# Preparation of the next group in sixteen pieces over a round trip, more streamed products beside scores and joins, a gate by banks

## The chip, the cores and the metric

The kernel runs on one core of one Trainium2 chip. The metric is the device time of one execution in microseconds (us). An execution has five engines and their queues: TensorE (PE, its weight loads PEld), VectorE (DVE), ScalarE (ACT), GpSimd (POOL), and SyncE (SP), which issues most of the DMA transfers.

## What is computed

One layer of a hybrid model on 256 tokens of width 2048, all in float32. A wide product `x @ w_in` gives the inputs of two mixers and two gates: a gated linear attention (GLA, 4 heads) and an RWKV-7 recurrence (16 heads of 64, forward and backward). Their outputs go through up-projections, are gated, summed and projected out, then comes a layer norm, and then a feed-forward layer with 16 experts that choose their tokens. Cut to what matters here:

```python
cols = x @ w_in                       # 2048 x 10592 weights
y_gla = gla_branch(q, k, v, g, af, ab, ...)    # ends in  * silu(g)
y_rw = rwkv_branch(rw_p, ...)
merged = sigmoid(gate_gla) * (y_gla @ w_up_gla) + sigmoid(gate_rw) * (y_rw @ w_up_rwkv)
x = layer_norm(ALPHA * x + merged @ w_out)
x = layer_norm(ALPHA * x + expert_choice_ffn(x, w_router, w1, w3, w2))

def rwkv_branch(...):                 # for each head, forward and backward
    w = exp(-0.606531 * sigmoid(w0 + tanh(xw) @ w_up));  a = sigmoid(a0 + xa @ a_up)
    kk = normalize(k * k_k);  k = k * (1 + (a - 1) * k_a);  a_vec, b_vec = -kk, kk * a
    # for each token:  S = S * w + (S @ a_vec) b_vec^T + v k^T ;  y = S @ r
```

## The kernel before

**Two phases.** The first phase computes everything up to the first layer norm. The second runs the experts, whose weights it reads from memory into rings of buffers that are taken from the first phase's pools when these close.

**Streamed products.** The dense products of the first phase are a list of jobs (`rw`, `lora`, `gqk`, `gv`, `gg`, `gate`, the up-projections, the output projection), in this order. For each block of 128 rows of weights, `split` (L241 on ScalarE, `tt` through L65 on VectorE) turns the raw float32 tile `wraw` into two reduced-precision parts `whi` and `wlo`, and three matmuls use them: L278 to L280 with 256 columns where the job gives its output transposed, L287 to L289 with 512 where it does not. In all jobs together 3888 such matmuls run. `wraw` has three buffers of two blocks; `fetch` (L224, on SyncE's queue) asks for the next pair of blocks as soon as the last one is split. `whi` and `wlo` have nine buffers each, and the splits run six blocks ahead. When a job's matmuls have ended, its `evac` generator is advanced by `drain`, one step for each block of the following job.

**The chain.** The two mixers are a chain of small matmuls and operations on VectorE and ScalarE: `rwkv_group` for four groups of four heads, then two GLA pairs. The chain is a generator, and `run_chain` sets the order of the program: at each `yield w` it lets the stream put `w` us worth of streamed products (by its own cost numbers) behind what the chain has just issued. All engines get their instructions in that order.

**One group.** `rwkv_group` starts with a transpose of the values (L774), then come the masked scores (matmuls L789, masks through L65 into `am`), eight halves with a `yield` after each. Then a first trip through device memory, the solution of small triangular systems on VectorE (the loop that ends at L870), and a second trip: SyncE stores the result to `sc2` (L873) and loads it back in another layout into `nt` (L878), both waiting for data. This second trip is the *round trip* here; `yield SUBST` (20.4 us of products) stands in it. Then VectorE transposes the blocks (L883), and the *joins* follow: matmuls L891, L898, L912 and L933, with copies and a second transpose (L902) between them. Then the *scan* over four chunks (L945 to L1003), and its output.

**What runs beside it.** `beside` wraps another generator so that `side(us)` advances it by `us` of its own yields. `side` is the preparation of the next group (`rwkv_prep`): matmuls L686, L693 and L703, then on ScalarE exponentials and logarithms (L688 to L742), on VectorE two running sums over time (L722 and L724), halves of the key product (L737), products (L745), and eight products of keys with decays, into `kr` (tag `t8`) and `nk` (tag `t8b`), with `yield 1.80` after each four. It is advanced in the triangle loop (`w * SPREAD`), in the round trip by `side(SIDE1)` with SIDE1 = 7.5, then in the scan (SIDE2), and a last `side(1e9)` at the group's end issues what is left, with its streamed products. `before` is the output part of the group before. Group 3 has no preparation to carry.

## Time and profile before

| What | Value |
|---|---|
| median of 3 runs | 1877.7 us (1876.88 to 1881.24) |
| the profiled execution | 1876.1 us, its span 1874.4 us |
| TensorE busy | 1607.3 us, 86% of the span, 11369 matmuls |
| VectorE busy | 775.6 us, 41%, 1407 instructions |
| ScalarE busy | 540.1 us, 29%, 1077 instructions |
| memory read, written | 543.20 MB, 16.78 MB; 299 GB/s over the span |
| transfers of the weights | `ring_a` 180, `ring` 139, `t8b` 39 of 1 MB each; `wraw` 112 of 512 KB and 96 of 256 KB on `w_in` |
| chain of work that ended last | DMA 41%, PE 32%, DVE 9%, ACT 2% |

The profile is one execution of the program, taken by the hardware profiler. A page lists busy times, the span in 40 slices, and groups of instructions; other views list the waits of an engine by the instruction that released it, the timeline of an engine, and tables by stretch. L-numbers are lines of the kernel. In a row, `out<-in` are the names of the tiles, and the "granted clock" is TensorE's as a share of 2.4 GHz, so that 0.50 is 1.2 GHz. The groups of rows further down say which view they are from.

### The profile page before, as it was taken

The numbers are of one execution on the slowest core, as the hardware profiler recorded it, in microseconds if no ns is written. First come the engines' busy times: TensorE is split into PE (matmuls) and PEld (weight loads), VectorE is DVE, ScalarE is ACT, GpSimd is POOL, SyncE is SP. The second block draws the span as 40 slices with busy tenths as digits, with TensorE's granted clock in tenths as the row PEclk, the third lists the DMA queues.
The fourth block names the chain that finished last, engine by engine and source line by source line (L and its number), as shares of the span: only waits on it lengthen the run. The fifth ranks groups of instructions, "written<-read, shape, count | busy, mean of one in ns | idle before, by whom it ended". The sixth has DMA issues, their size and how long they took to land.

```text
span 1874.4 us, 27915 instructions
## 1 busy us (share of the span) xinstructions
PE 1607.3 (86%) x11369; PEld 961.4 (51%) x11369; DVE 775.6 (41%) x1407; ACT 540.1 (29%) x1077; POOL 21.0 (1%) x45
## 2 busy tenths in 40 slices
PE   8999999989999999999796898668996679966684
PEld 8988877778777778888631233112331113411122
DVE  6777675757657885765531302111012110112114
ACT  5565454445546765544310001000010000100001
POOL 0000000000000000000000000000000000000001
PEclk9999999999999999999898899999999899998988
DMA  7757264552736658788899999999999999999997
GB/s 203 218 160 207 75 166 137 147 158 77 192 110 205 177 151 275 267 300 280 328 417 405 421 421 421 421 421 421 421 420 421 421 420 421 421 420 421 415 395 210
DMA packets 215426, 561.81 MB, mean 300 GB/s; under 512 B 49848, under 2 KB 110706, under 8 KB 171906
## 3 DMA queue, kind: packets, MB, share of 16 engines
q1 hardware_dynamic: 214000, 559.80, 80.9%
q8 instruction: 89, 1.46, 0.3%
q10 hardware_dynamic: 1298, 0.24, 0.1%
q14 instruction: 39, 0.32, 0.1%
HBM read 543.20 MB, written 16.78 MB: 299 GB/s over the span
## 4 chain that ended last, share of the span: by engine, by line
DMA 41%; PE 32%; DVE 9%; ACT 2%; issue 2%; SPq 1%; DVEq 0%; ACTq 0%
DMA ring_a<-in_w_dram 18%; DMA ring<-in_w_dram 17%; PE mm L287 6%; PE mm L288 5%; PE mm L289 5%; DMA t8b<-in_w_dram 5%; PE mm L1502 3%; PE mm L1462 2%; DVE wlo L65 2%; DVE t L65 2%; PE mm L278 2%; PE mm L279 1%; PE mm L280 1%; DVE t2p L65 1%; ACT whi L241 1%
## 5 line engine op out<-in xcount | busy, mean ns | idle before, releaser
L65 DVE TENSOR_TENSOR wlo<-wraw,whi 128x512 fp32r<-128x512 f32 (+2 forms) x480 | 308.5, 664 | 202.3 <-ACT whi L241 200.5
L241 ACT ACTIVATE whi<-wraw 128x512 fp32r<-128x512 f32 (+2 forms) x480 | 275.4, 606 | 181.3 <-DMA wraw<-in_w_in_dram 58.3
L278 PE MATMUL mm<-x,whi 128*128 128x256 f32 x688 | 207.6, 302 | 3.2 <-ACT whi L241 3.2
L1462 PE MATMUL mm<-ring_a,x 128*32 128x512 f32 x776 | 155.6, 671 | 57.4 <-DMA ring_a<-in_w_dram 57.4
L279 PE MATMUL mm<-x,whi 128*128 128x256 f32 x688 | 196.9, 286 | 0.0
L280 PE MATMUL mm<-x,wlo 128*128 128x256 f32 x688 | 196.8, 286 | 0.1
L1474 DVE TENSOR_SCALAR sig<-sig 64x512 f32<-64x512 f32 x16 | 6.8, 424 | 435.0 <-ACT sig L1472 435.0
L287 PE MATMUL mm<-whi,x 128*128 128x512 f32 x384 | 163.0, 424 | 4.6 <-DVE shd L65 4.6
L1502 PE MATMUL mm<-ring_a,hid 128*32 128x512 f32 (+1 forms) x560 | 152.0, 585 | 8.8 <-DMA ring_a<-in_w_dram 7.4
L1462 PE MATMUL mm<-ring,x 128*32 128x512 f32 x592 | 117.3, 687 | 48.7 <-DMA ring<-in_w_dram 48.6
L288 PE MATMUL mm<-wlo,x 128*128 128x512 f32 x384 | 154.1, 401 | 0.0
L289 PE MATMUL mm<-whi,x 128*128 128x512 f32 x384 | 153.4, 400 | 0.0
L65 DVE TENSOR_TENSOR x<-x,ax 128x512 f32<-128x512 f32 (+2 forms) x36 | 22.3, 626 | 289.8 <-PE ax L1509 289.8
L278 PEld LDWEIGHTS mm<-x,whi 128*128 128x128 f32 x688 | 133.7, 194 | 10.0 <-ACT whi L241 3.6
L279 PEld LDWEIGHTS mm<-x,whi 128*128 128x128 f32 x688 | 134.1, 195 | 2.3 <-issue 2.2
L280 PEld LDWEIGHTS mm<-x,wlo 128*128 128x128 f32 x688 | 133.9, 195 | 0.6 <-DVE wlo L65 0.6
L1472 ACT ACTIVATE sig<-mm 64x512 f32<-64x512 f32 x16 | 9.4, 588 | 407.8 <-PE mm L1462 407.8
L1502 PE MATMUL mm<-ring,hid 128*32 128x512 f32 (+2 forms) x456 | 120.7, 556 | 6.2 <-DMA ring<-in_w_dram 5.5
L1462 PEld LDWEIGHTS mm<-ring_a,x 128*32 128x32 f32 x776 | 30.1, 115 | 159.3 <-DMA ring_a<-in_w_dram 108.6
L1502 PEld LDWEIGHTS mm<-ring_a,hid 128*32 128x32 f32 x560 | 42.9, 113 | 107.7 <-issue 84.3
L1506 ACT ACTIVATE eo<-mm 128x512 f32<-128x512 f32 (+2 forms) x18 | 9.9, 550 | 295.4 <-PE mm L1502 282.5
L1462 PEld LDWEIGHTS mm<-ring,x 128*32 128x32 f32 x592 | 23.0, 118 | 132.7 <-DMA ring<-in_w_dram 91.9
(336 smaller groups left out, 2165.7 us busy)
## 6 DMA issues: line engine op xcount, KB each, us to landing
ring_a<-in_w_dram SPq DMA_DIRECT2D x180, 1024.0 KB
ring<-in_w_dram SPq DMA_DIRECT2D x139, 1024.0 KB
wraw<-in_w_in_dram SPq DMA_DIRECT2D x112, 512.0 KB
t8b<-in_w_dram SPq DMA_DIRECT2D x39, 1024.0 KB
wraw<-in_w_in_dram SPq DMA_DIRECT2D x96, 256.0 KB
wraw<-in_w_out_dram SPq DMA_DIRECT2D x24, 512.0 KB
ring_a<-in_w_dram SPq DMA_DIRECT2D x18, 512.0 KB
wraw<-in_w_up_rwkv_dram SPq DMA_DIRECT2D x16, 512.0 KB
```

The source lines that it names most:

```text
L65: dve.tensor_tensor(out_, a, b, op=op)
L241: act(hi, raw, AF.Copy)
L278: mm(o, whi[:, sl], hi(k), start=(st0 and cb % 2 == 0), stop=False, skip_group_check=True)
L279: mm(o, whi[:, sl], lo(k), start=False, stop=False, skip_group_check=True)
L280: mm(o, wlo[:, sl], hi(k), start=False, stop=st1, skip_group_check=True)
L287: mm(o, hi(k)[:, sl], whi, start=st0, stop=False)
L288: mm(o, hi(k)[:, sl], wlo, start=False, stop=False)
L289: mm(o, lo(k)[:, sl], whi, start=False, stop=st1)
L1462: mm(ps[32 * q:32 * q + 32, :], xe[:, kb, e4 * 32:e4 * 32 + 32], wt[q // 2][:, k, (q % 2) * 512:(q % 2) * 512 + 512], start=(kb == 0), sto ...
L1472: act(sg_[up_], ps[lo_], AF.Exp, scale=-1.0)
L1502: mm(ps[32 * e4:32 * e4 + 32, 0:m], hids[e4][:, fb % 4, fb // 4, :], wt[e4][:, j, c - c0:c - c0 + m], start=(fb == 0), stop=(fb == F // 12 ...
L1506: act(eo[:, 0:m], ps[:, 0:m], AF.Copy)
```

## The change

Five edits, and none adds or removes a streamed product, a transfer of weights or an operation of the preparation:

- The `yield SUBST + side(SIDE1)` in the round trip becomes sixteen yields of `SUBST / 16 + side(SIDE1 / 16)`, and SIDE1 goes from 7.5 to 20.4. The preparation, all but its last steps, is issued in that place, interleaved with the streamed products, in steps of 1.275 us.
- The last yields of the preparation go from 1.80 to 2.90 (two of them).
- The yield after each half of the scores goes from 0.41 to 0.75, and three yields between the joins from 1.00 to 1.60, 2.20 and 1.60.
- The step of the job `gg` that turns the gate into `silu` works on a whole bank (512 columns, in place in `shd`) instead of on halves (256 columns, in `shs`, with the product in `shd`): 2 x 4 steps of `drain` instead of 4 x 4 for each of the two jobs.
- In the preparation, the two ScalarE exponentials of `a_` are issued behind both matmuls instead of one behind each.

The diff:

```diff
-    SPREAD, SIDE1, SIDE2, POST, SUBST = 0.30, 7.50, 0.81, 1.35, 20.40
+    SPREAD, SIDE1, SIDE2, POST, SUBST, PIECES = 0.30, 20.40, 0.81, 1.35, 20.40, 16
...
             def ev(b, s=s):
-                for i in range(4):
-                    if i % 2 == 0:
-                        t = S([128, 2, T], "shd", 2)
-                    ge = S([128, T], "shs", 2)
-                    o = b[i // 2][:, i % 2 * T:i % 2 * T + T]
-                    act(ge, o, AF.Exp, scale=-1.0)
+                for i in range(2):
+                    ge = S([128, 512], "shd", 2)
+                    act(ge, b[i], AF.Exp, scale=-1.0)
                     yield
                     cap(ge)
                     yield
                     sigm(ge)
                     yield
-                    tt(t[:, i % 2, :], o, ge, OP.mult)
+                    tt(ge, b[i], ge, OP.mult)
                     yield
-                    if i % 2:
-                        c0 = s * 512 + i // 2 * 256
-                        load(gg_dram[c0:c0 + 256, :].rearrange("(a p) t -> p a t", p=128), t)
+                    c0 = s * 512 + i * 256
+                    load(gg_dram[c0:c0 + 256, :].rearrange("(a p) t -> p a t", p=128), ge.rearrange("p (a t) -> p a t", a=2))
...
         for p in range(2):
             mm(ps[:, p * T:p * T + T], lw[0:64, 1, p * 128:p * 128 + 128], xab[0:64, :], start=True, stop=True)
+        for p in range(2):
             act(a_[:, p, :], ps[:, p * T:p * T + T], AF.Exp, bias=na0[:, p0 + p:p0 + p + 1], scale=-1.0)
...
             tt(nk[:, d, :, :, 64:128], v4(k2), eN[:, :, :, inc], OP.mult)
-            yield 1.80
+            yield 2.90
...
-                    yield 0.41 + before(POST)
+                    yield 0.75 + before(POST)
...
-        yield SUBST + side(SIDE1)
+        for _ in range(PIECES):
+            yield SUBST / PIECES + side(SIDE1 / PIECES)
...
         act(cu[:, 0], pv, AF.Copy)
-        yield 1.00
+        yield 1.60
...
             dve.transpose(flat(us[32 * d:32 * d + 32]), flat(cu[96 * d:96 * d + 32, 1]))
-        yield 1.00
+        yield 2.20
...
         dve.tensor_copy(c1[tq[1]], pv[tq[1]])
-        yield 1.00
+        yield 1.60
```

Where the streamed products stand in TensorE's order, counted in the two programs (L-numbers of before; the groups are numbered from 0):

| Place | Before | After |
|---|---|---|
| ahead of the first scores, all | 804 | 825 |
| scores of group 0, one gap after another (L789) | 6, 9, 9, 6 | 12, 15, 15, 15 |
| group 0's round trip | L686, L686, L693, L703 at once, then 192 | L686, 12, L686, 12, L693, 24, L703, 144 |
| behind the joins L891, L898, L912, L933, group 0 | 9, 9, 12, 3 | 15, 18, 15, 6 |
| the same, group 1 | 6, 3, 6, 3 | 9, 9, 6, 3 |
| the same, group 2 | 9, 9, 9, 6 | 15, 18, 15, 6 |
| the same, group 3 | 6, 3, 6, 3 | 9, 9, 6, 3 |
| between the scan and the next L774, groups 0, 1, 2 | 42, 21, 45 | 9, 6, 3 |
| ahead of the last matmul of the second GLA pair (L1197), all | 2901 | 2958 |

VectorE in group 0's round trip, from the triangle to the transposes of the trip (L883 before, L881 after; `shs` and `shd` are the shift of an `rw` job), before:

```order
L65 TENSOR_TENSOR wlo<-wraw,whi 128x512 x12
L65 TENSOR_TENSOR shs<-ppad 128x256
L333 SCALAR_TENSOR_TENSOR shd<-shs,der,shd 128x256
L65 TENSOR_TENSOR wlo<-wraw,whi 128x512
L65 TENSOR_TENSOR shs<-ppad 128x256
L333 SCALAR_TENSOR_TENSOR shd<-shs,der,shd 128x256
L65 TENSOR_TENSOR wlo<-wraw,whi 128x512 x2
L65 TENSOR_TENSOR shs<-ppad 128x256
L333 SCALAR_TENSOR_TENSOR shd<-shs,der,shd 128x256
L65 TENSOR_TENSOR wlo<-wraw,whi 128x512
L883 STREAM_TRANSPOSE t_2196<-t_2196 64x512 x2
L65 TENSOR_TENSOR shs<-ppad 128x256
```

And after (`t_2460` is the preparation's `kkn`, `t2p` its decays, `t8b` its `nk`, `ld` its loaded inputs):

```order
L65 TENSOR_TENSOR shs<-ppad 128x256
L333 SCALAR_TENSOR_TENSOR shd<-shs,der,shd 128x256
L65 TENSOR_TENSOR wlo<-wraw,whi 128x512
L65 TENSOR_TENSOR shs<-ppad 128x256
L333 SCALAR_TENSOR_TENSOR shd<-shs,der,shd 128x256
L65 TENSOR_TENSOR wlo<-wraw,whi 128x512
L65 TENSOR_TENSOR t_2575<-t_2460,t2p 128x8x64
L65 TENSOR_TENSOR t_2575<-ld,t2p 128x8x64
L65 TENSOR_TENSOR t8b<-t_2511,t2p 128x8x64
L65 TENSOR_TENSOR t8b<-t_2461,t2p 128x8x64
L65 TENSOR_TENSOR wlo<-wraw,whi 128x512 x3
L881 STREAM_TRANSPOSE t_2271<-t_2271 64x512 x2
```

Four of the eight products with the decays, and the two halves and two products that they need, now stand ahead of the transposes of the trip, among the splits; before, all stood behind the joins.

ScalarE in the same place, before (L705 and L712 are the preparation's logarithm and exponential of the decays, L892 is the copy behind the first join):

```order
L698 ACTIVATE t_2214<-ld,prm 128x256 x2
L705 ACTIVATE t_2199<-t_2199,c_one 128x512 x2
L712 ACTIVATE t2p<-t_2199 128x8x64 x2
L332 ACTIVATE shd<-ppad,der 128x256
L241 ACTIVATE whi<-wraw 128x512 x11
L327 ACTIVATE ppad<-mm 128x2x256
L241 ACTIVATE whi<-wraw 128x512
L332 ACTIVATE shd<-ppad,der 128x256
L241 ACTIVATE whi<-wraw 128x512
L332 ACTIVATE shd<-ppad,der 128x256
L241 ACTIVATE whi<-wraw 128x512
L327 ACTIVATE ppad<-mm 128x2x256
```

And after, up to the second pass over the decays (L702, which ends a row ahead, and L709 are those two; the copy behind the first join is L890 and stands further down):

```order
L709 ACTIVATE t2p<-t_2274 128x8x64 x2
L241 ACTIVATE whi<-wraw 128x512
L713 ACTIVATE t_2324<-t_2324 128x512
L714 ACTIVATE t_2318<-t_2318,c_one 128x512
L241 ACTIVATE whi<-wraw 128x512
L723 ACTIVATE t_2324<-t_2324 128x512
L724 ACTIVATE t_2318<-t_2318 128x512
L327 ACTIVATE ppad<-mm 128x2x256
L241 ACTIVATE whi<-wraw 128x512
L729 ACTIVATE t2p<-t2p 128x520 x2
L735 ACTIVATE t_2461<-t_2318,der,prm 128x256 x2
L739 ACTIVATE t2p<-t2p 128x520 x2
```

The ten operations from L713 to L739 now stand ahead of the first join's copy, among the splits; before, they stood behind the joins (L716 to L742).

ScalarE in the job `gg0`, before (L416 is the exponential, L341 and L342 the logarithm and the exponential of `sigm`):

```order
L416 ACTIVATE shs<-mm 128x256
L241 ACTIVATE whi<-wraw 128x512 x2
L975 ACTIVATE av<-ax 64x4x64
L341 ACTIVATE shs<-shs,c_one 128x256
L342 ACTIVATE shs<-shs 128x256
L241 ACTIVATE whi<-wraw 128x512 x2
L975 ACTIVATE av<-ax 64x2x2x64
L416 ACTIVATE shs<-mm 128x256
L241 ACTIVATE whi<-wraw 128x512 x2
L341 ACTIVATE shs<-shs,c_one 128x256
L342 ACTIVATE shs<-shs 128x256
L241 ACTIVATE whi<-wraw 128x512 x2
```

And after (L413 is the exponential):

```order
L413 ACTIVATE shd<-mm 128x512
L241 ACTIVATE whi<-wraw 128x512 x2
L341 ACTIVATE shd<-shd,c_one 128x512
L342 ACTIVATE shd<-shd 128x512
L241 ACTIVATE whi<-wraw 128x512 x2
L413 ACTIVATE shd<-mm 128x512
L241 ACTIVATE whi<-wraw 128x512
```

One row on 512 columns stands for two on 256, and the second bank's exponential comes earlier among the splits.

## Rows read from the trace of the kernel before

**Rows 1.** The page's second part, the span in 40 equal slices: busy tenths.

```profile
PE   8999999989999999999796898668996679966684
...
DMA  7757264552736658788899999999999999999997
```

**Rows 2.** Waits of PE, 0 to 900 us: total us, times, longest us.

```profile
PE ax L789 <- DVE am L65: 6.8, 7, 2.0
...
PE mm L287 <- DVE shd L65: 4.6, 1, 4.6
...
PE ax L703 <- ACT t L698: 4.1, 3, 1.4
...
PE ax L789 <- DVE t8b L65: 3.2, 1, 3.2
```

**Rows 3.** Stretches: us; PE, PEld, DVE, ACT, POOL busy; clock; DMA; GB/s.

```profile
119.00:130.60 11.60, 10.77 (x95) 9.39 (x95) 11.26 (x21) 1.95 (x4) 0.11 (x1) 0.85 0.45 134
...
153.10:160.40 7.30, 5.28 (x13) 2.20 (x12) 6.24 (x14) 4.76 (x11) 0.00 (x0) 0.82 0.45 127
...
160.40:164.50 4.10, 4.10 (x21) 4.10 (x20) 3.73 (x7) 3.52 (x7) 0.00 (x0) 0.50 0.73 169
...
164.50:185.00 20.50, 20.50 (x173) 20.40 (x172) 12.21 (x22) 9.31 (x17) 0.00 (x0) 1.00 0.78 220
...
185.00:200.40 15.40, 13.53 (x435) 11.93 (x434) 7.27 (x15) 5.65 (x12) 0.00 (x0) 0.78 0.29 88
...
229.10:244.00 14.90, 11.11 (x99) 9.60 (x100) 13.81 (x26) 4.88 (x10) 0.00 (x0) 0.89 0.35 95
...
298.80:312.40 13.60, 12.10 (x420) 8.90 (x419) 6.28 (x13) 5.29 (x11) 0.00 (x0) 0.87 0.28 91
...
340.40:351.50 11.10, 9.59 (x83) 7.25 (x82) 10.44 (x19) 5.18 (x10) 0.00 (x0) 1.00 0.39 116
...
404.80:421.10 16.30, 13.37 (x435) 11.92 (x434) 6.73 (x13) 5.52 (x12) 0.00 (x0) 0.77 0.23 69
...
451.40:464.00 12.60, 9.38 (x90) 7.86 (x89) 12.29 (x24) 4.45 (x10) 0.52 (x1) 1.00 0.33 89
...
500.00:505.90 5.90, 5.82 (x14) 4.57 (x15) 0.62 (x2) 0.00 (x0) 0.00 (x0) 0.50 0.88 226
...
518.30:534.50 16.20, 13.45 (x419) 10.26 (x418) 6.68 (x13) 5.24 (x11) 0.00 (x0) 0.79 0.30 97
...
725.00:750.00 25.00, 25.00 (x111) 20.60 (x110) 11.55 (x20) 12.44 (x22) 0.00 (x0) 1.00 0.89 308
```

**Rows 4.** Timeline of DVE, 158 to 184 us: start, us, instruction, [idle before].

```profile
172.39 1.29 DVE L65 TENSOR_TENSOR wlo<-wraw,whi 128x512 fp32r<-128x512 f32 x2 [4.17 <-ACT whi L241]
...
183.30 0.71 DVE L883 STREAM_TRANSPOSE t<-t 64x512 f32<-64x512 f32 x1
```

**Rows 5.** Timeline of SyncE's queue, 155 to 190 us, in the same columns.

```profile
164.15 1.31 SPq L878 DMA_DIRECT2D t<-sc  x2
...
166.58 15.47 SPq L224 DMA_DIRECT2D wraw<-in_w_in_dram  x14
```

**Rows 6.** DVE's splits, 173.7-183.3, 284.3-297.6, 391.5-401.95 us: busy, mean ns, idle before.

```profile
L65 DVE TENSOR_TENSOR wlo<-wraw,whi 128x512 fp32r<-128x512 f32 x8 | 5.3, 687 | 1.7 <-ACT whi L241 1.6
...
L65 DVE TENSOR_TENSOR wlo<-wraw,whi 128x512 fp32r<-128x512 f32 x10 | 6.9, 691 | 6.5 <-ACT whi L241 6.4
...
L65 DVE TENSOR_TENSOR wlo<-wraw,whi 128x512 fp32r<-128x512 f32 x9 | 6.0, 689 | 4.5 <-ACT whi L241 4.5
```

**Rows 7.** DVE, 158 to 236 us, shapes apart: busy, mean ns, idle before.

```profile
L722 DVE TENSOR_TENSOR_SCAN t2p<-rstr,t2p 128x520 f32<-128x520 f32 x1 | 1.2, 1243 | 0.0
...
L737 DVE SCALAR_TENSOR_TENSOR t<-ld,prm,t 128x256 f32<-128x256 f32 x2 | 0.9, 470 | 0.0
...
L65 DVE TENSOR_TENSOR t8b<-t,t2p 128x512 f32<-128x512 f32 x4 | 2.6, 684 | 0.0
```

**Rows 8.** Timeline of ACT, 505 to 522 us, columns as in group 4.

```profile
505.96 0.63 ACT L241 ACTIVATE whi<-wraw 128x512 fp32r<-128x512 f32 x1 [6.47 <-DMA wraw<-in_w_in_dram]
```

## The prediction

> **What bounds the kernel now.** I read the slices of the page first [rows 1]. Up to about 900 us TensorE is busy almost without a break; after that the DMA engines are, with the experts' weights. The change touches the first part alone. Whatever that part loses or gains, the second part starts as much later or earlier: its weights go into buffers that come free when the first part ends. So I ask one thing: what TensorE does in the first part that is not matmul time at full clock. Its work there is fixed, since the same 3888 streamed products and the same chain matmuls run before and after. The time can move only by its waits and by stretches at half clock.
>
> The waits by releaser [rows 2] show where it waits: on the masked scores, on the preparation's squares, once on the gate's product, once on the first group's operands. The table by stretch [rows 3] gives their size: 119.0 to 130.6, 229.1 to 244.0, 340.4 to 351.5 and 451.4 to 464.0 are the scores of the four groups; 153.1 to 160.4 is the preparation of the next group, issued in one piece; 160.4 to 164.5 follows it at a granted clock of 0.50, which is 1.2 instead of 2.4 GHz; the four stretches from 185.0, 298.8, 404.8 and 518.3 are the joins, from the first join matmul to the first matmul of the scan. A streamed product costs 0.118 us where 256 columns move (20.50 us for 173) and 0.225 us where 512 do (25.00 for 111).
>
> A group is also a chain: scores, a first trip through memory, the triangle on VectorE, a second trip, transposes, joins, scan. From the end of the scores to the transposes it runs on VectorE, ScalarE and the queue of SyncE, and TensorE meets it again only at the first join. That decides what a saved wait is worth.
>
> **The change part by part.** My sum is made against the profiled execution, 1876.1 us with a span of 1874.4; the median of the runs shown is 1.6 us above it.
>
> *Products taken from the dense end.* By the order, 2901 products stand ahead of the last matmul of the second GLA pair before and 2958 now. Behind it they run dense at full clock. So 57 x 0.225 = 12.8 us of them leave that end: -12.8. What they cost where they go is in the next terms, which count the length of the chain itself.
>
> *First preparation.* It yields 2.2 us more, which is 21 products (2.5 us) ahead of the first scores. Those waited 3.2 us for VectorE's operands [rows 2]; two more splits of 0.69 us on VectorE push these back. I take +1.2 (bounds 0 and +2.5).
>
> *Scores.* Products between them: 30 to 57 in groups 0 and 1, 18 to 27 in group 2 (512 columns), 30 and 30 in group 3. Room in the stretches is what is not busy plus what the clock took: 0.8 + 1.7, 3.8 + 1.6, 1.5 and 3.2 us [rows 3]. The products need 3.2, 3.2, 2.0 and 0. So they nearly fill holes: +0.7, -0.4, +0.5, -0.3, in sum +0.5 (bounds -3 and +5). In group 1 VectorE is busy 13.8 of 14.9 us, so the stretch can't shrink much.
>
> *The round trip.* This term has the widest bounds. What goes for certain is the lump on TensorE: 7.3 us with 2.0 idle and a clock of 0.82, then 4.1 us at half clock [rows 3]. If TensorE were the end here, group 0 would gain 2.0 + 1.0 + 2.1 = 5.1 us; groups 1 and 2 have the same lump, and I take 13 for the three as the bound. But the first join needs the transposes (L883 before), which stand in VectorE's queue behind everything that is put into the trip. In group 0 they start at 183.30 [rows 4], 19 us after SyncE issued their loads at 164.15 [rows 5], and TensorE's join starts at 185.0, only 1.7 us later. In between, a split waited until 172.39 for a weight load, because SyncE's queue stood at the trip's own waits and this load was issued at 166.58 [rows 4, 5]. The change moves onto VectorE, ahead of the transposes: two scans, two halves of the key product, two products, and four of the eight products with the decays, 2 x 1.24 + 2 x 0.47 + 6 x 0.68 = 7.5 us [rows 7]. The scans fit into the idle time before the load lands; 5.0 us stand behind it, where VectorE was idle for 1.7 us only [rows 6]. So group 0's transposes start 3 us later, and ScalarE, which gets ten more operations there and waits for the same load in the middle of them, adds about one: +4. In groups 1 and 2 VectorE was idle for 6.5 and 4.5 us behind the load [rows 6], so 7.5 and 5.0 + 0.8 (the gate's sigmoid now falls there) find nearly enough: +1 and +1.5. Together +6.5 for these groups; the upper bound is all 7.5 us in each with ScalarE's share, +30 (below). TensorE, without its lump, reaches the join some 5 us earlier than now and waits there: a new wait on the transposes takes the place of the lump.
>
> In that trip the rows show the order of the queue: the transposes of group 0 start at 183.30, in their place behind the splits, though their loads were issued 19 us before [rows 4, 5]. The Trainium skill, "TensorE: Matmul & The Clock Gate", section on the array's architectural detail, calls the queues of ScalarE and VectorE strictly first in, first out. By that rule this part of the change costs time, as in the sum; if a ready transpose could pass the preparation, the term would be the bound of -13.
>
> *The gate's sigmoid by banks.* It halves its steps, 16 turns to 8, so the product that reads the bank comes before the job that reuses it. The wait of 4.6 us goes [rows 2], and with it the 5.9 us at clock 0.50 behind it [rows 3], 2.9 us. What is late next is the chain: that wait lies in group 3's trip, where ScalarE waited 6.47 us for a weight load until 505.96 [rows 8], whatever TensorE did, with the join at 518.3. VectorE has two operations fewer there. I take -0.5 (bounds -7.5 and 0): the 4.6 us reappear at the join.
>
> *Joins.* Idle 1.9 + 1.5 + 2.9 + 2.8 = 9.1 us, and the clock (0.78, 0.87, 0.77, 0.79) took 3.4 + 1.8 + 3.7 + 3.4 = 12.3. Products go from 33, 18, 33, 18 to 54, 27, 54, 27: 2 x 21 x 0.118 + 2 x 9 x 0.225 = 9.0 us. They fill the idle time. With the clock full the term is 9.0 - 21.4 = -12.4; with the clock as now it is 0. A wait of several us now stands right ahead of them, and after the one of 4.6 us the clock was at 0.50 [rows 3]. I take half: -6.
>
> *Scan and tails.* VectorE has 7.5 us less beside the scan: -2 (bounds -4 and 0; no row above prices it, the nearest is the idle time of the joins). Between scan and next scores stood 42, 21 and 45 products that covered the last decay products; these are done earlier, and 9, 6 and 3 stand there now: -3.9, -3.4, -4.6, in sum -11.9 (bounds -12 and -8). Next is then the transpose of the values, which needs a load from long before.
>
> Sum: -12.8 + 1.2 + 0.5 + 6.5 - 0.5 - 6 - 2 - 11.9 = -25.0, so **1876.1 - 25.0 = 1851 us**.
>
> **Rivals.** *The trip stays covered*: VectorE and ScalarE keep up, the join doesn't wait, the clock stays full. Then the trip is -13, the gate -7.5, the joins -12.4, and the rest as above: 1876 - 58 = 1818. For it: VectorE idles 6.5 and 4.5 us behind the load in groups 1 and 2. Against: group 0's 1.7 us [rows 6].
>
> *The chain takes it back*: trip +13, joins 0, scan 0; the others stay: 1.2 + 0.5 + 13 - 0.5 - 11.9 - 12.8 = -10.5, 1866. For it: 1.7 us of slack in group 0.
>
> *The preparation becomes the end, and the kernel slower*: ScalarE's part of the moved preparation is about 6 us (ten operations, at the 0.63 us of its split of the same width [rows 8]); if it and VectorE's 7.5 run one after the other behind the load, a trip is 13 us longer, 40 us in three, and with joins at half clock the sum is 1876 + 10 = 1886. It decides from about 10 us per trip. Against: the two engines overlap everywhere else.
>
> *It doesn't reach the chip as meant*: were the waits to move and nothing else, 1876. The order speaks against it, since the products really stand elsewhere.
>
> **How the numbers follow.** Forecast 0.62 (its own range 1840 to 1861, from half the bounds of trip and joins), covered trip 0.09, chain takes it back 0.16, no effect 0.06, slower 0.07. The range 1834 to 1868 leaves out most of the covered trip, no effect and slower. A measurement of this kernel can tell about 0.3%, 5.6 us. Faster by more than that: 0.62 + 0.09 + 0.13 = 0.84; the same: 0.06 + 0.03 = 0.09; slower 0.07.
>
> **What would show it.** In the profile after: no wait of TensorE on the gate's `shd` and none on the preparation's squares; a wait of 4 to 10 us before the first join on VectorE's transposes in groups 0 to 3, which is the key sign; the wait on masked scores down from 6.8 to about 3 us; fewer half-clock slices between 150 and 175; the joins' idle time under 4 us in sum. The phase of the experts' weights keeps its length and starts about 25 us earlier. If the join doesn't wait, the covered trip is right; if the wait exceeds 12 us in each group, the sum fails towards slower.

## The result and the profile after

The median of four runs after is 1860.0 us (1853.3 to 1861.9), that of the four runs of before that go with them 1878.3 us. The ratio is 0.9889, with a 95% interval of 0.9867 to 0.9911: some 21 us faster. The profiled execution took 1860.8 us with a span of 1859.1, 15.3 us less than the span of before. All readings below are from these two executions, so they explain 15.3 us; the rest of the 21 lies between executions of the same kernel. L-numbers of the changed kernel are two to four lower than those of before from the gate's job on.

The slices of the page (TensorE, DMA) read as [rows 1]: one phase of TensorE, then one of DMA.

```profile
PE   8999899989999999999796998668986679966784
...
DMA  7766464463736557887999999999999999999996
```

The waits of TensorE, 0 to 900 us (total us, times, longest), to be read against [rows 2]:

```profile
PE ax L889 <- DVE t L881: 20.9, 4, 8.6
PE mm L278 <- ACT whi L241: 5.1, 2, 3.5
...
PE ax L786 <- DVE am L65: 2.8, 3, 1.4
...
PE ax L786 <- DVE t8b L65: 0.5, 1, 0.5
```

The wait on the masked scores is down from 6.8 to 2.8 us, that on the first scores' operands from 3.2 to 0.5. The gate's product and the preparation's squares are gone from the list. In their place stands one new wait of 20.9 us, ahead of the first join (L889) on VectorE's transposes (L881), once in each group: 8.6, 3.3, 5.5 and 3.6 us.

The stretches, in the columns of [rows 3]. The scores are those from 119.9, 235.7, 342.7 and 453.1; 158.7 to 167.3 is the preparation's start in the first trip; 188.0 to 197.4 holds the new wait of group 0 (8.59 us of it is that wait).

```profile
119.90:134.00 14.10, 12.02 (x107) 10.78 (x107) 13.41 (x24) 5.48 (x11) 0.23 (x2) 0.88 0.56 156
158.70:167.30 8.60, 8.60 (x58) 7.12 (x57) 8.39 (x18) 5.50 (x13) 0.00 (x0) 1.00 0.64 184
...
188.00:197.40 9.40, 0.81 (x53) 0.70 (x56) 9.14 (x17) 2.01 (x4) 0.11 (x1) 0.62 0.71 207
...
235.70:246.70 11.00, 10.97 (x111) 9.91 (x110) 9.78 (x18) 4.52 (x9) 0.00 (x0) 1.00 0.37 114
...
342.70:353.50 10.80, 10.80 (x90) 8.37 (x89) 9.33 (x17) 4.52 (x9) 0.00 (x0) 1.00 0.30 87
...
453.10:465.00 11.90, 11.22 (x92) 8.66 (x92) 10.52 (x19) 6.88 (x13) 0.52 (x1) 1.00 0.32 91
```

The stretch with the preparation runs at a granted clock of 1.00 now (0.82 and then 0.50 in [rows 3]).

The joins, from the first matmul that has to wait for the transposes to the first matmul of the scan, in the same columns, before (the stretches of [rows 3] end up to 1.6 us later, behind the scan's first matmuls):

```profile
185.04:198.81 13.77, 12.05 (x418) 10.90 (x417) 7.09 (x15) 4.90 (x10) 0.00 (x0) 0.75 0.32 98
298.83:311.39 12.56, 11.11 (x403) 8.15 (x402) 6.25 (x13) 4.33 (x9) 0.00 (x0) 0.86 0.31 99
404.79:419.82 15.03, 12.10 (x419) 10.77 (x418) 6.73 (x13) 5.15 (x11) 0.00 (x0) 0.80 0.21 60
518.31:533.47 15.16, 12.49 (x403) 9.49 (x402) 6.67 (x13) 4.25 (x9) 0.00 (x0) 0.77 0.31 102
```

And after:

```profile
196.73:209.76 13.03, 13.03 (x434) 12.22 (x434) 7.62 (x15) 5.03 (x10) 0.00 (x0) 0.86 0.40 120
302.10:315.44 13.34, 12.87 (x407) 9.97 (x407) 7.62 (x15) 5.08 (x10) 0.00 (x0) 0.87 0.40 119
410.87:424.92 14.05, 13.35 (x434) 12.55 (x434) 8.53 (x17) 6.28 (x12) 0.00 (x0) 0.84 0.47 139
516.46:530.50 14.04, 13.29 (x407) 10.07 (x407) 8.05 (x16) 6.86 (x13) 0.00 (x0) 0.88 0.48 139
```

TensorE is idle in them for 1.9 us in sum (8.8 before), and the clock takes 7.5 us (11.7 before). In sum they last 54.46 instead of 56.52 us, 2.1 us less, with 9.0 us more of streamed products in them.

At the head of the joins TensorE stands still:

```profile
187.90 0.25 PE L889 MATMUL ax<-t,moff 32*32 32x32 f32 x4
196.74 1.92 PE L889 MATMUL ax<-t,moff 32*32 32x32 f32 x124 [8.59 <-DVE t L881]
```

These are TensorE's rows around the first join of group 0 (start, us, instruction, [idle before]). The first four matmuls need only what came straight from memory; the next one waits 8.59 us for the transposes.

Where the 15.3 us are is seen best from the places where the stages start and end. Each number is a difference of starts and ends of instructions in the two traces, in us; "triangle's end" is the `memset` of L871 (L868 after), "joins" are from the transposes' start to the last matmul of L933 (L931):

| Stage | Group 0 | Group 1 | Group 2 | Group 3 | Sum of changes | Forecast |
|---|---|---|---|---|---|---|
| up to the first scores | 115.3 to 118.8 | | | | +3.4 | +1.2 |
| scores | 14.5 to 15.3 | 14.9 to 11.5 | 11.7 to 11.4 | 13.1 to 12.5 | -3.6 | +0.5 |
| scores' end to triangle's end | 28.8 to 30.8 | 29.3 to 28.4 | 27.5 to 29.2 | 29.6 to 28.8 | +2.0 | not in the sum |
| round trip, to the transposes' start | 24.8 to 31.2 | 24.7 to 26.3 | 22.9 to 27.4 | 23.9 to 21.9 | +12.4, group 3 -2.0 | +6.5, -0.5 |
| joins | 14.7 to 12.8 | 12.3 to 12.7 | 16.4 to 13.2 | 14.7 to 13.3 | -6.1 | -6 |
| scan and tail, to the next group | 30.6 to 26.4 | 29.9 to 28.1 | 32.6 to 29.2 | | -9.4 | -2 - 11.9 |
| group 3's scan to the last streamed product | | | | 388.5 to 376.4 | -12.1 | -12.8 |
| from there to the end | | | | 953.7 to 953.7 | 0.0 | 0 |

The forecast's joins began at the first join matmul, not at the transposes. TensorE came to that matmul 1.7, 1.2, 2.9 and 0.8 us after the transposes' start before, and 0.8 us after it in every group now. So, counted to the matmul, the three trips are only 8.9 us longer (5.4, 1.1 and 2.3) where the table has 12.4, and 3.6 us of the table's -6.1 are this.

The chain of the four groups is only 3.2 us shorter than before (532.2 to 529.0 at the last join): what it gains in scores, joins and tails it pays in the round trip. The rest of the gain is the dense end, from which 57 products were taken.

Why the trip is longer is on VectorE and ScalarE. VectorE in group 0's trip (start, us, instruction, [idle before]):

```profile
178.55 0.69 DVE L65 TENSOR_TENSOR wlo<-wraw,whi 128x512 fp32r<-128x512 f32 x1 [4.49 <-ACT whi L241]
...
184.09 0.48 DVE L333 SCALAR_TENSOR_TENSOR shd<-shs,der,shd 128x256 f32<-128x256 f32 x1 [1.68 <-ACT shd L332]
...
192.85 1.28 DVE L65 TENSOR_TENSOR t8b<-t,t2p 128x512 f32<-128x512 f32 x2
194.06 1.89 DVE L65 TENSOR_TENSOR wlo<-wraw,whi 128x512 fp32r<-128x512 f32 x3
195.97 1.44 DVE L881 STREAM_TRANSPOSE t<-t 64x512 f32<-64x512 f32 x2
```

ScalarE and SyncE's queue in the same place:

```profile
177.88 0.63 ACT L241 ACTIVATE whi<-wraw 128x512 fp32r<-128x512 f32 x1 [5.70 <-DMA wraw<-in_w_in_dram]
...
180.46 1.16 ACT L729 ACTIVATE t2p<-t2p 128x520 f32<-128x520 f32 x2
181.52 1.08 ACT L735 ACTIVATE t<-t,der,prm 128x256 f32<-128x256 f32 x2
182.50 1.15 ACT L739 ACTIVATE t2p<-t2p 128x520 f32<-128x520 f32 x2
183.56 0.50 ACT L332 ACTIVATE shd<-ppad,der 128x256 f32<-128x256 f32 x1
```

```profile
170.68 1.31 SPq L875 DMA_DIRECT2D t<-sc  x2
172.09 15.64 SPq L224 DMA_DIRECT2D wraw<-in_w_in_dram  x10
```

The triangle ends at 164.82. As in [rows 5], SyncE stands at the trip's own loads (170.68, the row of L875) before it can ask for the next weights (172.09); so ScalarE's split waits 5.70 us until 177.88 and VectorE's until 178.55, 13.7 us after the triangle, just as before (13.9). From there to the transposes it was 10.9 us before and is 17.4 now. Of the 6.5 us more, 4.9 are the operations that were put there, and 1.4 is additional idle time: ScalarE's passes over the decays (180.46 to 183.65) stand ahead of the shift's operation at 183.56, for which VectorE waits 1.68 us. In all that time the transposes stand behind.

### The profile page after: what moved, and what is told of

Its sections match the earlier page's. It is cut to its first block, busy times and chain, and to the rows that moved or that the text cites. A ratio compares the mean times of both kernels' runs of the same rounds, so it can differ in the third digit from the quotient of the medians.

```text
span 1859.1 us, 27901 instructions
## 1 busy us (share of the span) xinstructions
PE 1601.8 (86%) x11369; PEld 956.3 (51%) x11369; DVE 774.7 (42%) x1399; ACT 535.6 (29%) x1065; POOL 21.6 (1%) x45
## 4 chain that ended last, share of the span: by engine, by line
DMA 43%; PE 32%; DVE 10%; ACT 2%; issue 2%; SPq 1%; DVEq 0%; ACTq 0%
DMA ring_a<-in_w_dram 18%; DMA ring<-in_w_dram 18%; PE mm L287 5%; DMA t8b<-in_w_dram 5%; PE mm L288 5%; PE mm L289 5%; PE mm L1500 3%; DVE wlo L65 3%; PE mm L1460 2%; DVE t L65 2%; PE mm L278 1%; DMA wraw<-in_w_in_dram 1%; PE mm L279 1%; PE mm L280 1%; DVE t2p L65 1%
## 5 line engine op out<-in xcount | busy, mean ns | idle before, releaser
L278 PEld LDWEIGHTS mm<-x,whi 128*128 128x128 f32 x688 | 132.7, 193 | 13.8 <-ACT whi L241 5.7
L1460 PEld LDWEIGHTS mm<-ring,x 128*32 128x32 f32 x592 | 22.9, 117 | 133.4 <-DMA ring<-in_w_dram 94.3
```

The costliest lines, as they stand in the source:

```text
L278: mm(o, whi[:, sl], hi(k), start=(st0 and cb % 2 == 0), stop=False, skip_group_check=True)
L1460: mm(ps[32 * q:32 * q + 32, :], xe[:, kb, e4 * 32:e4 * 32 + 32], wt[q // 2][:, k, (q % 2) * 512:(q % 2) * 512 + 512], start=(kb == 0), sto ...
```

## The experiments

Two theories. **Products**: the change gains by products that leave the dense end for places in which the chain waits anyhow; spreading the preparation over the trip gains nothing by itself, because it puts work ahead of the transposes in VectorE's queue. **Spread**: the gain is the lump that goes from the trip, and the longer yields matter little. Within the first, the trip's length may come from the order of VectorE's queue (**queue**) or from the weight load that SyncE asks for too late (**late load**). The ratios, each to the runs of before beside it:

| Run | Median us | Ratio | 95% interval |
|---|---|---|---|
| the change | 1860.0 | 0.9889 | 0.9867 to 0.9911 |
| `e1_products` | 1863.2 | 0.9905 | 0.9884 to 0.9925 |
| `e2_spread` | 1892.8 | 1.0066 | 1.0043 to 1.0089 |
| `e3_banks` | 1877.2 | 0.9980 | 0.9965 to 0.9994 |
| `e4_lump` | 1861.1 | 0.9880 | 0.9853 to 0.9907 |
| `e5_hoist` | 1839.7 | 0.9782 | 0.9763 to 0.9801 |
| `e6_late_nt` | 1846.4 | 0.9819 | 0.9802 to 0.9837 |
| `e7_side7` | 1862.8 | 0.9914 | 0.9899 to 0.9929 |
| `e8_both` | 1832.7 | 0.9752 | 0.9736 to 0.9767 |
| `e9_both_side7` | 1844.1 | 0.9805 | 0.9790 to 0.9820 |
| `e10_before_both` | 1878.7 | 0.9987 | 0.9972 to 1.0002 |

### The longer yields alone

To the kernel before:

```diff
-            yield 1.80
+            yield 2.90
...
-                    yield 0.41 + before(POST)
+                    yield 0.75 + before(POST)
...
-        yield 1.00
+        yield 1.60
...
-        yield 1.00
+        yield 2.20
...
-        yield 1.00
+        yield 1.60
```

> The kernel before with the longer yields alone (scores 0.75, joins 1.60, 2.20, 1.60, last steps of the preparation 2.90); the preparation still stands in one piece at the start of the round trip. By the order 3039 products stand ahead of the last matmul of the second GLA pair, 138 more than before (after: 57 more). Theory 'products': the gain of the change is products that leave the dense end for places where the chain waits anyhow, so this edit alone gains too: 138 x 0.225 = 31 us leave the dense end, about half of it comes back as a longer chain, because what is put behind the last steps of the preparation has no wait to fill; about 1862 us, ratio 0.992. Theory 'spread': the gain is the lump that goes from the round trip, so this edit alone gains little: 1872 us, ratio 0.997 or above.

Measured: 1863.2 us, ratio 0.9905. This edit alone gives 18 us. In its trace group 3's last join ends at 549.5 (532.2 before, +17.3), and from there to the last streamed product it takes 361.5 us (388.5 before, -27.0): nearly two thirds of what leaves the dense end comes back as a longer chain. Of that, 10.0 us are in the tails, where the last products of the preparation, each with a longer yield, still stand here, and 9.2 us between the scores' end and the triangle's end; the trips are 3.5 us shorter. Which of the yields pays wasn't tried apart. Theory "products" is borne out, theory "spread" falls.

### The spread trip alone

To the kernel before:

```diff
-    SPREAD, SIDE1, SIDE2, POST, SUBST = 0.30, 7.50, 0.81, 1.35, 20.40
+    SPREAD, SIDE1, SIDE2, POST, SUBST, PIECES = 0.30, 20.40, 0.81, 1.35, 20.40, 16
...
-        yield SUBST + side(SIDE1)
+        for _ in range(PIECES):
+            yield SUBST / PIECES + side(SIDE1 / PIECES)
```

> The kernel before with the round trip in sixteen pieces and SIDE1 at 20.4 alone; all yields as before. 2871 products stand ahead of the last GLA matmul, 30 fewer than before. Theory 'products': the dense end gets 30 x 0.225 = 6.8 us longer, the three trips get 12 us longer by VectorE's queue, and the tails 9 us shorter: +8, about 1886 us, ratio 1.004, with a wait on the transposes ahead of the first joins of about 25 us in sum. Theory 'spread': 1862 us, ratio 0.992.

Measured: 1892.8 us, ratio 1.0066. The part that gives the change its name makes the kernel before some 12 us slower. The waits of TensorE in its trace:

```profile
PE ax L892 <- DVE t L884: 24.7, 3, 11.0
PE mm L287 <- DVE shd L65: 6.6, 1, 6.6
```

The transposes (L884 here) hold up the first join for 24.7 us in three groups, as expected. In the profiled execution (1897.6 us) the dense end is 13.2 us longer; the 30 products that went back to it are 6.8 of them by their price, the rest is open. The gate's product holds TensorE up as in [rows 2], for longer.

### The gate by banks alone

To the kernel before, the edit of the job `gg` as in the diff of the change:

```diff
-                for i in range(4):
...
+                for i in range(2):
+                    ge = S([128, 512], "shd", 2)
+                    act(ge, b[i], AF.Exp, scale=-1.0)
```

> The kernel before with the gate's sigmoid by banks alone. The products stand in the order as before. Both theories: the wait of 4.6 us on the gate's product goes; as the prediction has it, it reappears at the first join of group 3, net 0 to -1, ratio 0.9995. If it doesn't reappear, up to -7.5 with the half clock behind it, ratio 0.996.

Measured: ratio 0.9980, interval 0.9965 to 0.9994, some 4 us faster and so between the two values. The wait on the gate's product is gone from its list, and this stands there (none of it in the kernel before):

```profile
PE ax L887 <- DVE t L879: 8.8, 2, 6.4
```

Here L887 is the first join and L879 are the transposes. The 6.4 us are in group 3, so the 4.6 us did come back as a wait at a join, as the prediction says. Where the 4 us come from stays open: the profiled execution (1881.8 us) is above the median and doesn't show them.

### All but the spread

To the changed kernel:

```diff
-    SPREAD, SIDE1, SIDE2, POST, SUBST, PIECES = 0.30, 20.40, 0.81, 1.35, 20.40, 16
+    SPREAD, SIDE1, SIDE2, POST, SUBST, PIECES = 0.30, 7.50, 0.81, 1.35, 20.40, 1
```

> The changed kernel with the round trip in one piece again and SIDE1 at 7.5; the longer yields, the gate by banks and the order of the two exponentials stay. 3039 products stand ahead of the last GLA matmul. Theory 'products': as the first of these runs, less the gate's share, 1860 us, so that spreading over the trip gives nothing on top of the longer yields. Theory 'spread': 1871 us, 10 us above the changed kernel.

Measured: ratio 0.9880 (0.9853 to 0.9907), the same as the change (0.9889) within the intervals. Spreading adds nothing on top of the longer yields. The order of the two exponentials is in both kernels and wasn't run by itself. The waits of TensorE in its trace (an execution of 1850.4 us, the fastest of the six):

```profile
PE ax L700 <- ACT t L695: 5.8, 3, 2.3
PE ax L889 <- DVE t L881: 4.9, 3, 4.3
```

With the lump back, the wait on the preparation's squares is back (L700 on L695, 5.8 us), and the wait on the transposes is 4.9 instead of 20.9 us (4.3 of it in group 3). The change trades one for the other.

### The same steps, spread

To the changed kernel:

```diff
-    SPREAD, SIDE1, SIDE2, POST, SUBST, PIECES = 0.30, 20.40, 0.81, 1.35, 20.40, 16
+    SPREAD, SIDE1, SIDE2, POST, SUBST, PIECES = 0.30, 7.50, 0.81, 1.35, 20.40, 16
```

> The changed kernel with SIDE1 at 7.5 and the sixteen pieces kept: the same steps of the preparation as before stand in the round trip, but spread over it; the rest stands in the scan and behind it. 3039 products stand ahead of the last GLA matmul, as in the run with the trip in one piece. It tells the lump from the amount. If the lump on TensorE costs time by itself, this is 3 to 6 us below the run with one piece: 1856 us, ratio 0.986. If only VectorE's queue counts, the same as with one piece, 1861 us; if spread steps delay the transposes, 1865 us.

Measured: ratio 0.9914 (0.9899 to 0.9929), 1862.8 us. Not better than with one lump (0.9880); the intervals just meet. Ahead of the first joins TensorE waits

```profile
PE ax L889 <- DVE t L881: 14.9, 4, 4.6
```

So this shows no cost of the lump by itself; what TensorE doesn't spend in it, it spends waiting for the transposes, even where only the preparation's first steps stand in the trip.

### The transposes nine pieces into the trip

To the changed kernel:

```diff
-        for _ in range(PIECES):
-            yield SUBST / PIECES + side(SIDE1 / PIECES)
         flat = lambda t: t.rearrange("p m c -> p (m c)")
-        for d in (1, 0):
-            sl = slice(64 * d, 64 * d + 64)
-            dve.transpose(flat(nt[sl, 1 - d]), flat(nt[sl, d]))
+        for n in range(PIECES):
+            if n == 9:
+                for d in (1, 0):
+                    sl = slice(64 * d, 64 * d + 64)
+                    dve.transpose(flat(nt[sl, 1 - d]), flat(nt[sl, d]))
+            yield SUBST / PIECES + side(SIDE1 / PIECES)
```

> The changed kernel with the two transposes of the round trip issued after nine of the sixteen pieces instead of after all; products, preparation and loads stand as in the changed kernel. Theory 'queue': the joins wait because the transposes stand in VectorE's queue behind the preparation and the splits, though their data is there. Then the wait of 20.9 us ahead of the first joins falls under 6, the three trips get 12 us shorter, about 1848 us, ratio to before 0.982. Theory 'late load': the trip is as long as the split that waits for its weight load and what must follow it; TensorE's own work takes the place of the wait, at most 4 us are gained, 1856 us.

Measured: 1839.7 us, ratio 0.9782: 20 us below the change, where theory "queue" expected 12. VectorE in its trip of group 0:

```profile
174.62 0.69 DVE L65 TENSOR_TENSOR wlo<-wraw,whi 128x512 fp32r<-128x512 f32 x1 [3.32 <-ACT whi L241]
...
181.41 1.42 DVE L881 STREAM_TRANSPOSE t<-t 64x512 f32<-64x512 f32 x2
...
190.67 1.29 DVE L65 TENSOR_TENSOR t8b<-t,t2p 128x512 f32<-128x512 f32 x2
```

The transposes run at 181.41, 19.0 us after the triangle's end (31.2 in the change), and the decay products of the preparation follow them. Ahead of the first joins there is no wait of TensorE in any group. The joins, from the first join matmul to the first of the scan:

```profile
185.40:203.70 18.30, 14.12 (x439) 13.02 (x438) 14.96 (x29) 6.28 (x12) 0.11 (x1) 0.81 0.66 202
292.20:305.30 13.10, 11.67 (x413) 9.01 (x412) 10.18 (x20) 6.37 (x12) 0.11 (x1) 1.00 0.58 172
395.00:409.80 14.80, 12.26 (x441) 11.03 (x439) 13.11 (x25) 9.68 (x18) 0.00 (x0) 1.00 0.67 190
495.20:509.50 14.30, 12.18 (x413) 9.20 (x412) 9.47 (x19) 9.34 (x18) 0.00 (x0) 1.00 0.64 197
```

Group 0's are longer than behind the wait in the change (18.3 for 13.0 us): VectorE now has the rest of the preparation there (15.0 us busy for 7.6), and TensorE waits 2.67 us for the second transpose. The other three differ by less than 0.8 us, and the clock is 1.00 in them where it was 0.84 to 0.88. From the triangle's end to the first join the four trips are 21.3 us shorter than in the change: all of the wait of 20.9 went, because TensorE comes to the join only 4.0 to 6.0 us after the transposes' start, held by nothing but its own work. The expectation of 12 was too small. The order of the queue is the cause of the wait; the form of "late load" that leaves at most 4 us to be gained falls.

### The trip's loads behind three pieces

To the changed kernel:

```diff
-        for d in range(2):
-            load(nt[64 * d:64 * d + 64, d], sc2[32768 * d:32768 * d + 32768].rearrange("(m p c) -> p m c", p=64, c=32))
-        for _ in range(PIECES):
+        for n in range(PIECES):
+            if n == 3:
+                for d in range(2):
+                    load(nt[64 * d:64 * d + 64, d], sc2[32768 * d:32768 * d + 32768].rearrange("(m p c) -> p m c", p=64, c=32))
             yield SUBST / PIECES + side(SIDE1 / PIECES)
```

> The changed kernel with the loads of the round trip issued behind three of the sixteen pieces, so that SyncE's queue asks for the next weights before it stands at the trip's own wait; transposes at the end as in the changed kernel. Theory 'late load': the split that waited 4.5 to 5.7 us for its weights doesn't wait any more, each trip gets some 4 us shorter, 12 to 16 in sum, about 1847 us, ratio 0.982. Theory 'queue': the idle time moves to the splits behind, which stand at TensorE's pace, and the trips get 1 to 2 us shorter each, about 1856 us.

Measured: 1846.4 us, ratio 0.9819: 13 us below the change. SyncE's queue, ScalarE's split that waited before, and the wait ahead of the first joins:

```profile
164.44 1.77 SPq L224 DMA_DIRECT2D wraw<-in_w_in_dram  x2
167.29 1.32 SPq L877 DMA_DIRECT2D t<-sc  x2
```

```profile
169.20 0.63 ACT L241 ACTIVATE whi<-wraw 128x512 fp32r<-128x512 f32 x1 [0.47 <-DMA wraw<-in_w_in_dram]
```

```profile
PE ax L890 <- DVE t L882: 10.8, 4, 5.6
```

SyncE asks for weights at 164.44, before it stands at the trip's loads (167.29), and the split waits 0.47 us instead of 5.70. The wait ahead of the joins falls from 20.9 to 10.8 us, so both causes are real: the stall sets when the backlog of VectorE begins, and the queue's order lets the transposes wait for all of it.

### Both

To the changed kernel, the two edits above with the transposes at piece 11:

```diff
+        for n in range(PIECES):
+            if n == 3:
+                for d in range(2):
+                    load(nt[64 * d:64 * d + 64, d], sc2[32768 * d:32768 * d + 32768].rearrange("(m p c) -> p m c", p=64, c=32))
+            if n == 11:
+                for d in (1, 0):
+                    sl = slice(64 * d, 64 * d + 64)
+                    dve.transpose(flat(nt[sl, 1 - d]), flat(nt[sl, d]))
+            yield SUBST / PIECES + side(SIDE1 / PIECES)
```

> The changed kernel with the loads of the round trip behind three pieces and the transposes after eleven. Theories 'queue' and 'late load' together: no wait ahead of the first joins but for TensorE's own work, trips 20 us shorter in sum, about 1842 us, ratio 0.979. If the later loads arrive too late for the transposes at their new place, VectorE's queue stands there and the splits behind it, and it is no better than with the transposes alone.

Measured: 1832.7 us, ratio 0.9752: by the ratios some 26 us below the change, and the fastest of all. In group 0's trip VectorE's split doesn't wait, and the transposes run 18.4 us after the triangle's end (162.81):

```profile
171.73 0.67 DVE L65 TENSOR_TENSOR wlo<-wraw,whi 128x512 fp32r<-128x512 f32 x1
...
181.18 1.45 DVE L882 STREAM_TRANSPOSE t<-t 64x512 f32<-64x512 f32 x2
```

TensorE reaches the join at 183.40, after the transposes, and in the other groups too it comes 4.2 to 4.9 us after their start; the trip is set by its own products now. The two gains overlap: 20 and 13 us apart, 26 together.

### Both, without the moved preparation

To the kernel of the run above:

```diff
-    SPREAD, SIDE1, SIDE2, POST, SUBST, PIECES = 0.30, 20.40, 0.81, 1.35, 20.40, 16
+    SPREAD, SIDE1, SIDE2, POST, SUBST, PIECES = 0.30, 7.50, 0.81, 1.35, 20.40, 16
```

> The kernel of the run before (loads of the round trip behind three pieces, transposes after eleven) with SIDE1 at 7.5: the preparation is no longer moved into the round trip, only its first steps stand there, as in the kernel before. Theory 'queue': moving the preparation into the trip pays as soon as the transposes are not behind it, since its last products then don't stand in the tails; so this run is slower than the one with 20.4, by about 10 us: 1843 us, ratio to before 0.981. Rival: the spread gives nothing even so, 1833 us, ratio 0.975.

Measured: 1844.1 us, ratio 0.9805. With the transposes out of the way, moving the preparation into the trip is worth 0.9805 to 0.9752, some 10 us; with the transposes behind it, nothing (`e4_lump` against the change), and without the longer yields it costs 12 us (`e2_spread`).

### The order alone

To the kernel before, only the places of the trip's loads and transposes (three and eleven sixteenths of the trip's products); the preparation's first steps stay in one piece:

```diff
+        for n in range(PIECES):
+            if n == 3:
+                for d in range(2):
+                    load(nt[64 * d:64 * d + 64, d], sc2[32768 * d:32768 * d + 32768].rearrange("(m p c) -> p m c", p=64, c=32))
+            if n == 11:
+                for d in (1, 0):
+                    sl = slice(64 * d, 64 * d + 64)
+                    dve.transpose(flat(nt[sl, 1 - d]), flat(nt[sl, d]))
+            yield SUBST / PIECES + (0.0 if n else side(SIDE1))
```

> The kernel before, with nothing of the change but the place of the trip's loads (behind three sixteenths of the trip's products) and of its transposes (behind eleven sixteenths); the preparation's first steps stay in one piece at the start. Theory 'queue': before, TensorE was busy in all of the trip behind the lump and met the transposes 1.7 us late in group 0 at most, so there is nothing to gain: 1876 us, ratio 0.999, and the gain of the order is a gain on top of the change only. Rival: the transposes and loads were late in the kernel before too; then 1860 us, ratio 0.990.

Measured: ratio 0.9987 (0.9972 to 1.0002), no change. The transposes do start earlier, 16.6 us after the triangle's end in group 0 (24.8 before), but TensorE is at the first join only 7.1 us after their start (7.1 to 9.2 in the four groups), and from the triangle's end to that join the four trips take 1.0 us more than before. In the kernel before, TensorE met the transposes in time; the order of the queue only costs where the change has put work in front of them.

## Why the prediction was right, and where it was not

The time was forecast at 1851 us, 25 us less, with a range of 1834 to 1868; 1860 us came out, 15 us less in the profiled execution, 18 by the medians, 21 by the ratio. The main mechanisms were right, and the signs named ahead are in the profile: no wait on the gate's product or the squares, a wait on the transposes at the first join of all four groups, the wait on the masked scores at 2.8 us, the joins' idle time at 1.9 us, and no half clock between 150 and 175 (1.00 for 0.86). The wait on the transposes was to be 4 to 10 us; it is 8.6, 3.3, 5.5 and 3.6, so two of four are below that. The experts' phase keeps its length and starts 15 us earlier, not 25.

In the profiled execution the sum is 9.7 us short of the forecast. By the forecast's own stretches the trips, the joins, the tails, the first preparation and the stretch to the triangle's end each came out 2 to 4 us worse, and the scores 4.1 us better; the time lies in the range because the range is wide, and not because each term was right.

**Dense end**, -12.8: right in size (-12.1). The price of 0.225 per product is nearly that of `e4_lump`, 31.3 us less for 138 products, 0.227 each; `e1_products` has 27.0 for the same 138, 0.196 each. What came out more sharply than the text had it: this term is most of the gain of the profiled execution, because the chain's other terms nearly cancel.

**Round trip**, +6.5: right in sign and cause, mis-sized. It is +12.4 to the transposes' start (6.4, 1.6 and 4.4 where 4, 1 and 1.5 stood), and +8.9 to TensorE's join; I had not counted that TensorE used to come later than the transposes. The step that failed is the subtraction of slack: I took VectorE's idle time behind the weight load [rows 6] as room for the moved operations. It stands between splits that wait for ScalarE, and only part of it was of use: in group 0 the idle time behind the load grew from 1.6 to 3.0 us instead of being used up, since ScalarE got its own part of the preparation in the same place. In group 2 VectorE still idles 3.0 us (0.87 and 2.14) of the 4.5 behind the load, and then works without a break from 400.63 to the transposes at 410.11. There the room lay ahead of the work, not under it. In group 1, where most of it stood, it did serve: 6.5 us of idle time became 3.3, and the transposes start 1.6 us later where I had said 1. That a transpose can't pass what is queued ahead of it was the right rule, and the Trainium skill ("TensorE: Matmul & The Clock Gate", section on the array's architectural detail) has VectorE strictly first in, first out. The traces agree: with nothing moved but the place of the transposes, `e5_hoist` starts them 19.0 instead of 31.2 us after the triangle.

**Scores**, +0.5: wrong in sign, -3.6. Nearly all of it is group 1 (14.9 to 11.5 us), of which I said that it can't shrink because VectorE was busy 13.8 of 14.9 us. VectorE is busy 9.8 of 11.0 there now. Part of what filled it was not the scores' work. Groups of VectorE in that stretch of before, 229.1 to 244.0, shapes apart:

```profile
L65 DVE TENSOR_TENSOR t8b<-t,t2p 128x512 f32<-128x512 f32 x2 | 1.3, 684 | 0.0
...
L65 DVE TENSOR_TENSOR t<-t,t2p 128x512 f32<-128x512 f32 x1 | 0.7, 685 | 0.0
L65 DVE TENSOR_TENSOR t<-ld,t2p 128x512 f32<-128x512 f32 x1 | 0.7, 685 | 0.0
```

These are four of the preparation's products with the decays, 2.7 us, which ran over from the tail into the scores; in the same stretch of after there is none. The longer yields alone and the spread alone each bring these scores down to 11.8 and 11.7 us too. I had taken the load of one engine in a stretch as fixed while the change moved it.

**Joins**, -6: -2.1 by the stretch that the sum used, so mis-sized; the table's -6.1 starts earlier and matches by chance. The 9.0 us of products are there, but of the idle time 6.9 us went where all 9.1 were to go, and the clock gave back 4.2 us where 6.2 were to come. What keeps the clock down in the joins stays open: in `e5_hoist` three of the joins without a wait ahead run at 1.00, but the fourth at 0.81, and in the kernel before all four ran at 0.75 to 0.86 without such a wait.

**Scan and tails**, -13.9: -9.4. The products are gone from the tails by the order (the last of their three prices is 42 x 0.118 = 5.0, not 4.6), and so far as the scores of group 1 got shorter, part of this term is booked there. Another part went to the clock: from the scan's first matmul to the next group it was 1.00, 1.00 and 0.93 before, and is 1.00 and then, in groups 1 and 2,

```profile
315.43:342.12 26.69, 26.37 (x323) 19.60 (x324) 14.35 (x30) 9.12 (x21) 0.11 (x1) 0.94 0.34 100
424.91:452.52 27.61, 27.30 (x359) 23.61 (x360) 14.10 (x30) 8.11 (x19) 0.00 (x0) 0.88 0.25 76
```

which takes 2.7 us more than before; the forecast had no clock in this term.

**First preparation**, +1.2: +3.4, above its bound of 2.5, but not all of it is the change. In `e2_spread`, `e3_banks` and `e10_before_both` TensorE has the same matmuls in the same order up to there as before, and the first scores start at 117.4, 118.5 and 117.3 us, not at 115.3; the mean of the four is 117.1, and the change's 118.8 is 1.7 us above it. The stretch between the scores and the triangle's end, +2.0, was not in the sum. It comes with the longer yields: they alone make it 9.2 us longer (`e1_products`), and in group 0 it is 30.7 us there and 30.8 in the change, but 28.8 in `e2_spread`. By which path they do so wasn't tried.

**Gate by banks**, -0.5: alone some -4 (`e3_banks`), inside the bounds; its wait did reappear at the join. The -2.0 of group 3's trip can't be put down to it: the banks alone make that trip 0.6 us longer, the longer yields alone 1.3 us shorter.

The rivals: the *covered trip* (1818) falls with the 20.9 us of waiting. *The chain takes it back* (1866) was closer than the forecast, since the profiled execution (1860.8) lies 5 us below it and 10 above the forecast: its trip of +13 is what was measured to the transposes; joins and scores then gave more than it allowed. A *slower* kernel was right of the trip's edit taken alone (`e2_spread`).

## What to carry to other kernels

When work is spread into a wait, put the operation that ends the wait ahead of it in its engine's queue, at the point where its data has landed, and issue a load that must wait behind those that needn't: here this order was worth some 26 us on top of the change, and nothing without it. An idle time in a list is room for new work only if it lies behind that work's inputs and ahead of the next deadline; place the slack on the time axis before subtracting it. And price the parts of a change apart: of this one, longer yields alone gave 18 us, and the part that it is named after cost 12 by itself and paid 10 only with the trip's order put right.

## What the runs showed of the hardware

In these runs a DMA issue that waits holds up what stands behind it in SyncE's queue: behind the trip's loads the next weights were asked for 7.3 us after the triangle's end (172.09 against 164.82), ahead of them 2.8 us after it (164.44 against 161.61), and the split's wait fell from 5.70 to 0.47 us. I had seen the stall in [rows 5] but not expected that moving the trip's own loads later would pay 13 us.
